# The k-slices of the split weights at 528 bytes instead of 512

## The chip, the cores and the metric

The kernel runs on one core of one Trainium2 chip. What counts is the device time of one execution in microseconds, as the median of several runs. A profile is one further execution, recorded instruction by instruction.

## The reference, cut to what matters

The program computes two residual layers on 512 positions of 1,024 channels in float32: an even layer (a chunked state-space scan beside differential attention), an odd layer (a diagonal state-space model beside latent attention), and a gated feed-forward after each. Nearly all of the work is projections `h @ w` with large weight matrices:

```python
def swiglu(x, wg, wu, wd):
    return (jax.nn.silu(x @ wg) * (x @ wu)) @ wd

for i in range(DEPTH):
    hn = rms_norm(h, norm_mix[i])
    h = h + (even_mixer(hn, ...) if i % 2 == 0 else odd_mixer(hn, ...))
    h = h + swiglu(rms_norm(h, norm_ffn[i]), ffn_gate[i], ffn_up[i], ffn_down[i])
return rms_norm(h, norm_final)
```

## The kernel before

Activations lie transposed: a tile of 128 channels by 512 positions, 2,048 bytes in each partition. The eight tiles of a layer's input are each held as a high part and a low part (`x0h`, `x0l` to `x7h`, `x7l`) whose sum is the float32 value, and the weights are split in the same way, so that three matmuls in the faster float32r format (high by high, high by low, low by high) stand for one float32 product.

The work comes in units. A unit is one block of 128 output channels (a few have 32 or 16): its weights are `nk` k-slices of `cw` columns, mostly 8 slices of 128. `wload` (line 154) brings the weights of one or more units into a tile `raw` with one DMA on SyncE's queue. `wsplit` (line 161) makes two tiles: `whi`, a cast on ScalarE (line 169), and `wlo`, raw minus high on VectorE (line 170). Both are allocated as 1,024 floats (4,096 bytes) from a pool `whl` with two buffers for each name, and slice k of 128 columns starts at 512 k bytes. In the last stage some weights are used twice and are kept in tiles of their own (`kh`, `kl`, 896 floats). `mm3` (line 173) issues three matmuls for each slice, lines 178, 179 and 180, with the slice as the stationary operand and 512 (at the end 256) positions as the moving one. In `v_part` (line 738) and `values` (line 1355) the slices are the moving operand.

`drive` (line 244) sets the order: before a unit's matmuls are issued, `prep` (line 192) issues the split of the next unit, so that ScalarE and VectorE work on it beside TensorE. `compute` (line 205) issues the matmuls and the unit's evacuation from PSUM, and then what is due from a queue of steps that are put off by a number of units. `even`, `ffn` and `odd` (lines 479, 936, 1217) give the units of the layers and the steps between them.

Memory is given out pool by pool in the order in which `setup` (line 370) and the layers open them. A pool `pad` of 320 floats, of which one is set by a memset on GpSimd (line 380), stands ahead of the residual tiles, the activation tiles, `raw` and `whl`; the layers' own pools come behind `whl`.

Of the kernel before, what the change touches and what calls it, by code (L numbers as in the profile page):

```python
# [9 lines left out]
F32 = mybir.dt.float32  # L10
F32R = mybir.dt.float32r
# [3 lines left out]
ALU = mybir.AluOpType  # L15
# [3 lines left out]
P = 128  # L19
# [2 lines left out]
KD = D // P  # L22
EPS = 1e-6
PAD, PAD5 = 320, 112
FFN = 2816
NH = FFN // P
MAGIC = 12582912.0
# [94 lines left out]
class Trunk:  # L122
# [38 lines left out]
    def wsplit(self, raw, o, nk, cw, keep=None):  # L161

        nc = self.nc
        n = nk * cw
        if keep is None:
            hi, lo = (self.t(self.whl, [P, 1024], x, F32R) for x in ("whi", "wlo"))
        else:
            hi, lo = (self.t(self.finp, [P, n], f"{x}{keep}", F32R) for x in ("kh", "kl"))
        nc.scalar.copy(out=hi[:, :n], in_=raw[:, o:o + n])  # L169
        nc.vector.tensor_tensor(out=lo[:, :n], in0=raw[:, o:o + n], in1=hi[:, :n].bitcast(F32), op=ALU.subtract)  # L170
        return [x[:, :n].rearrange("p (k c) -> p k c", k=nk) for x in (hi, lo)]

    def mm3(self, ps, hi, lo, k0, xs, m, start=True, stop=True):
        nc = self.nc
# [195 lines left out]
    def setup(self):  # L370
        nc, ctx = self.nc, self.ctx
        cp = self.cp = self.pool(ctx, "const")
        self.stp = self.pool(ctx, "stp")
        pad = self.pool(ctx, "pad")
        self.hp = self.pool(ctx, "hp")
        self.xnp = self.pool(ctx, "xnp")
        self.tmp = self.pool(ctx, "tmp")
        self.wraw = self.pool(ctx, "wraw", 2)
        self.whl = self.pool(ctx, "whl", 2)
        nc.gpsimd.memset(self.t(pad, [P, PAD], "pad")[:, 0:1], 0.0)  # L380
        self.pp = {n: self.pool(ctx, "ps_" + n, b, PSUM) for n, b in (("mm", 2), ("sc", 2), ("tp", 2), ("po", 2))}
        self.n_unit = 0
        self.raws, self.kept = {}, {}
        self.queue, self.held = [], None
        self.cst_sb = self.t(cp, [P, NCST], "cst")
        self.par_sb = self.t(cp, [P, NPAR], "par")
        nc.scalar.dma_start(out=self.par_sb, in_=self.a["par"])
        nc.scalar.dma_start(out=self.cst_sb, in_=self.a["cst"])
        self.ident = self.cst("ident")
        self.ones = self.t(cp, [P, P], "ones")  # L390
        nc.gpsimd.memset(self.ones, 1.0)
        self.mrow = self.t(cp, [1, P], "mrow", BF16)
        nc.gpsimd.memset(self.mrow[:, 0:64], 1.0)
        nc.gpsimd.memset(self.mrow[:, 64:128], 0.0)
        self.nrow = self.t(cp, [1, 64], "nrow", BF16)
        nc.gpsimd.memset(self.nrow, NEG)
        self.rowb = self.t(cp, [P, 32], "rowb")
        nc.scalar.dma_start(out=self.rowb, in_=self.a["rowp"].broadcast_to([P, 32]))
        self.sel = self.t(cp, [64, 16], "sel", F32R)
        nc.scalar.copy(out=self.sel, in_=self.cst("sel")[0:64, :])  # L400
        self.halfpi = self.t(cp, [P, 1], "hpi")
        nc.gpsimd.memset(self.halfpi, math.pi / 2)
        self.h = [self.t(self.hp, [P, T], f"h{i}") for i in range(KD)]
        self.xn = [None] * KD
# [1216 lines left out]
```

## Time and profile before

| | |
|---|---|
| median of 3 runs | 1480.8 us (1479.17 to 1481.18) |
| profiled execution | 1481.41 us |
| its span, from the first to the last instruction | 1479.6 us |
| mean granted TensorE clock | 0.986 |
| busy: TensorE, VectorE, ScalarE, GpSimd | 96%, 64%, 45%, 17% |
| chain that ended last: TensorE, VectorE, ScalarE, GpSimd | 74%, 18%, 3%, 2% |

Busy time is the union of an engine's instructions. TensorE's matmuls are pipelined: one is recorded as 0.39 us long while the next one starts 0.23 us after it, so the distance of the starts says more than the length. Weight loads are recorded apart, as PEld. The chain is followed back from the last instruction: at each step to what released it, or to the instruction before it on its engine.

### The profile page before, as it was taken

The page shows a single profiled execution, that of the slowest core. Times are in us where ns is not written, and L with a number is a line of the kernel's source. Part 1 is how long each engine was busy: PE and PEld are TensorE (multiplying, and loading weights), DVE is VectorE, ACT ScalarE, POOL GpSimd, SP SyncE. Part 2 cuts the span into 40 slices and gives each one's busy share as a digit, 9 for nine tenths or more (in the row PEclk, how much of TensorE's full clock was granted, in tenths as well). Part 3 has the DMA queues.
Part 4 walks back from the last instruction along what each step waited for, and adds up shares of the span by engine and source line. Part 5 has one row for each costly group of instructions (what it writes and reads, how often), then busy time and mean ns, then how long its engine had stood idle before and what let it go on. Part 6 is the DMA issues. An engine that isn't in the chain of part 4 may idle for free.

```text
span 1479.6 us, 18488 instructions
## 1 busy us (share of the span) xinstructions
PE 1426.2 (96%) x7043; PEld 1155.1 (78%) x7043; DVE 954.1 (64%) x1992; ACT 661.5 (45%) x1198; POOL 256.9 (17%) x206
## 2 busy tenths in 40 slices
PE   7999999999999999999999997789999999999997
PEld 5877877788878877888888886666688888888887
DVE  6987788777664999774634469886664433443453
ACT  5658766767544334334223453256453322222342
POOL 0234511000002210011011213523221100100111
PEclk9999999999999999999999998889999999999999
DMA  5221121112212222223222221020122232323221
GB/s 179 78 73 58 61 82 44 59 57 72 86 58 85 102 86 86 86 86 107 96 103 87 98 86 38 24 75 2 62 109 85 89 112 86 108 77 114 86 100 57
DMA packets 20248, 119.80 MB, mean 81 GB/s; under 512 B 2368, under 2 KB 3008, under 8 KB 9024
## 3 DMA queue, kind: packets, MB, share of 16 engines
q1 hardware_dynamic: 18864, 116.86, 22.9%
q10 hardware_dynamic: 1296, 1.76, 0.4%
q8 instruction: 55, 0.90, 0.3%
q14 instruction: 33, 0.27, 0.1%
HBM read 116.52 MB, written 2.10 MB: 80 GB/s over the span
## 4 chain that ended last, share of the span: by engine, by line
PE 74%; DVE 18%; ACT 3%; POOL 2%; issue 2%; DMA 1%; SPq 0%; ACTq 0%; DVEq 0%; POOLq 0%
PE mm L178 14%; PE mm L180 14%; PE mm L179 13%; PE sc L180 7%; PE sc L179 7%; PE sc L178 7%; DVE wlo L170 3%; PE sc L1397 1%; PE sc L813 1%; POOL xs L281 1%; PE po L842 1%; DVE qsw L608 1%; PE mm L750 1%; PE po L1425 1%; PE sc L812 1%
## 5 line engine op out<-in xcount | busy, mean ns | idle before, releaser
L169 ACT CAST whi<-raw 128x1024 fp32r<-128x1024 f32 (+5 forms) x231 | 223.9, 970 | 568.6 <-PE mm L179 331.3
L170 DVE TENSOR_TENSOR wlo<-raw,whi 128x1024 fp32r<-128x1024 f32 (+5 forms) x231 | 266.8, 1155 | 44.2 <-ACT whi L169 31.6
L281 POOL TENSOR_TENSOR gt<-gt,rbc 128x512 f32<-128x512 f32 x44 | 76.3, 1734 | 572.6 <-ACT gt L952 572.6
L957 DVE TENSOR_TENSOR gt<-mm,gt 128x512 f32<-128x512 f32 x44 | 30.3, 690 | 111.3 <-PE mm L180 107.9
L281 POOL TENSOR_TENSOR sacc<-sacc,sq 128x512 f32<-128x512 f32 x29 | 45.4, 1566 | 300.5 <-issue 232.7
L951 DVE TENSOR_TENSOR gt<-sc,rbc 128x512 f32<-128x512 f32 x44 | 30.3, 689 | 88.9 <-PE sc L180 88.9
L180 PE MATMUL mm<-x0h,wlo 128*128 128x512 f32 (+2 forms) x91 | 37.2, 409 | 12.4 <-DVE wlo L170 12.4
L178 PE MATMUL mm<-x0h,whi 128*128 128x512 f32 (+2 forms) x91 | 39.9, 438 | 6.1 <-ACT x0h L343 5.4
L972 DVE TENSOR_TENSOR h<-h,mm 128x512 f32<-128x512 f32 x20 | 13.7, 687 | 44.0 <-PE mm L180 44.0
L768 ACT ACTIVATE qsw<-mm 32x512 f32<-32x512 f32 x64 | 37.7, 589 | 3.1 <-DVE qraw L764 2.3
L972 DVE TENSOR_TENSOR h<-h,sc 128x512 f32<-128x512 f32 x20 | 13.7, 686 | 38.9 <-PE sc L180 38.8
L178 PE MATMUL mm<-x1h,whi 128*128 128x512 f32 (+2 forms) x91 | 36.7, 403 | 1.8 <-ACT x1h L343 1.8
L952 ACT ACTIVATE gt<-gt 128x512 f32<-128x512 f32 x44 | 27.6, 628 | 22.9 <-DVE gt L951 22.9
L180 PE MATMUL mm<-x1h,wlo 128*128 128x512 f32 (+2 forms) x91 | 37.3, 410 | 0.0
L180 PE MATMUL mm<-x2h,wlo 128*128 128x512 f32 (+2 forms) x91 | 37.2, 408 | 0.0
L178 PE MATMUL mm<-x7h,whi 128*128 128x512 f32 (+2 forms) x95 | 37.1, 391 | 0.0
L180 PE MATMUL mm<-x7h,wlo 128*128 128x512 f32 (+2 forms) x95 | 37.1, 391 | 0.0
L179 PE MATMUL mm<-x7l,whi 128*128 128x512 f32 (+2 forms) x95 | 37.0, 390 | 0.0
L179 PE MATMUL mm<-x0l,whi 128*128 128x512 f32 (+2 forms) x91 | 36.8, 405 | 0.2 <-DVE x0l L344 0.2
L179 PE MATMUL mm<-x2l,whi 128*128 128x512 f32 (+2 forms) x91 | 37.0, 407 | 0.0
L179 PE MATMUL mm<-x1l,whi 128*128 128x512 f32 (+2 forms) x91 | 36.8, 404 | 0.2 <-DVE x1l L344 0.2
L178 PE MATMUL mm<-x3h,whi 128*128 128x512 f32 (+2 forms) x91 | 36.8, 405 | 0.0
(938 smaller groups left out, 4385.5 us busy)
## 6 DMA issues: line engine op xcount, KB each, us to landing
raw<-in_f_dram SPq DMA_DIRECT2D x52, 1024.0 KB, 4.8
raw<-in_w_dram SPq DMA_DIRECT2D x35, 1024.0 KB, 4.8
raw<-in_f_dram SPq DMA_DIRECT2D x16, 896.0 KB, 4.5
raw<-in_w_dram SPq DMA_DIRECT2D x8, 512.0 KB, 3.6
h<-in_xt_dram SPq DMA_DIRECT2D x8, 256.0 KB, 6.8
raw<-in_w_dram SPq DMA_DIRECT2D x2, 640.0 KB, 3.9
out_dram<-otm SPq DMA_DIRECT2D x4, 256.0 KB, 2.5
out_dram<-otm ACTq DMA_DIRECT2D x4, 256.0 KB, 2.9
```

What stands on the lines that cost most here:

```text
L169: nc.scalar.copy(out=hi[:, :n], in_=raw[:, o:o + n])
L170: nc.vector.tensor_tensor(out=lo[:, :n], in0=raw[:, o:o + n], in1=hi[:, :n].bitcast(F32), op=ALU.subtract)
L178: nc.tensor.matmul(ps, lhsT=hi[:, k, :m], rhs=xh, start=start and j == 0, stop=False)
L179: nc.tensor.matmul(ps, lhsT=hi[:, k, :m], rhs=xl, start=False, stop=False)
L180: nc.tensor.matmul(ps, lhsT=lo[:, k, :m], rhs=xh, start=False, stop=stop and j == n - 1)
L281: self.nc.gpsimd.tensor_tensor(out=out, in0=x, in1=y, op=op)
L608: V.scalar_tensor_tensor(out=acc, in0=xr[:, 1 + k:1 + k + T], scalar=self.par("cw", 12 * k + j), in1=acc, op0=ALU.mult, op1=ALU.add)
L768: A.activation(out=sw[c * 32:(c + 1) * 32, :], in_=ps[d * 32:(d + 1) * 32, :], func=AF.Identity, scale=scale)
L951: V.tensor_tensor(out=gt, in0=ps, in1=E["rbc"], op=ALU.mult)
L952: A.activation(out=gt, in_=gt, func=AF.Silu)
L957: V.tensor_tensor(out=gt, in0=ps, in1=gt, op=ALU.mult)
L972: V.tensor_tensor(out=self.h[i], in0=self.h[i], in1=ps, op=ALU.add)
```

## The change

A constant `WGAP` of 4 floats, 16 bytes, is added behind each k-slice in `whi` and `wlo`: slices of 128 columns lie 528 bytes apart, those of 256 columns 1,040. The low parts start 32 floats, 128 bytes, into their tile. The tiles grow to 1,056 and 1,088 floats. ScalarE and VectorE write through a view in three dimensions that leaves the gaps out. The kept tiles stay as they were, written through a view of the same contiguous memory. A new pool `padw` of 320 floats behind `whl`, with a memset of one value on GpSimd, makes the two pools together 2,048 bytes longer than `whl` was.

```diff
+WGAP = 4
@@ wsplit
         if keep is None:
-            hi, lo = (self.t(self.whl, [P, 1024], x, F32R) for x in ("whi", "wlo"))
+            w = nk * (cw + WGAP)
+            hi, lo = (self.t(self.whl, [P, 1024 + 8 * WGAP + s], x, F32R)[:, s:s + w].rearrange(
+                "p (k c) -> p k c", k=nk)[:, :, :cw] for x, s in (("whi", 0), ("wlo", 8 * WGAP)))
         else:
-            hi, lo = (self.t(self.finp, [P, n], f"{x}{keep}", F32R) for x in ("kh", "kl"))
-        nc.scalar.copy(out=hi[:, :n], in_=raw[:, o:o + n])
-        nc.vector.tensor_tensor(out=lo[:, :n], in0=raw[:, o:o + n], in1=hi[:, :n].bitcast(F32), op=ALU.subtract)
-        return [x[:, :n].rearrange("p (k c) -> p k c", k=nk) for x in (hi, lo)]
+            hi, lo = (self.t(self.finp, [P, n], f"{x}{keep}", F32R).rearrange("p (k c) -> p k c", k=nk)
+                      for x in ("kh", "kl"))
+        src = raw[:, o:o + n].rearrange("p (k c) -> p k c", k=nk)
+        nc.scalar.copy(out=hi, in_=src)
+        nc.vector.tensor_tensor(out=lo, in0=src, in1=hi.bitcast(F32), op=ALU.subtract)
+        return hi, lo
@@ setup
         nc.gpsimd.memset(self.t(pad, [P, PAD], "pad")[:, 0:1], 0.0)
+        nc.gpsimd.memset(self.t(self.pool(ctx, "padw"), [P, 320], "padw")[:, 0:1], 0.0)
```

## Rows read from the trace of the kernel before

**Rows 1.** The page: busy time by engine; the chain that ended last, by engine and line.

```profile
PE 1426.2 (96%) x7043; PEld 1155.1 (78%) x7043; DVE 954.1 (64%) x1992; ACT 661.5 (45%) x1198; POOL 256.9 (17%) x206
...
PE 74%; DVE 18%; ACT 3%; POOL 2%; issue 2%; DMA 1%; SPq 0%; ACTq 0%; DVEq 0%; POOLq 0%
PE mm L178 14%; PE mm L180 14%; PE mm L179 13%; PE sc L180 7%; PE sc L179 7%; PE sc L178 7%; DVE wlo L170 3%; PE sc L1397 1%; PE sc L813 1%; POOL xs L281 1%; PE po L842 1%; DVE qsw L608 1%; PE mm L750 1%; PE po L1425 1%; PE sc L812 1%
```

**Rows 2.** Busy time by stretch: length, then busy and instructions by engine, TensorE clock, DMA.

```profile
core 0: us, PE busy (x) PEld busy (x) DVE busy (x) ACT busy (x) POOL busy (x), PEclk, DMA share, GB/s
100.00:300.00 200.00, 194.72 (x1080) 155.44 (x1078) 157.45 (x320) 147.92 (x271) 51.69 (x36) 0.97 0.17 59
1200.00:1300.00 100.00, 100.00 (x443) 82.87 (x442) 37.62 (x42) 25.18 (x30) 10.82 (x6) 1.00 0.27 94
```

**Rows 3.** Matmuls in order of time, second feed-forward: start and length in us.

```profile
1305.04 0.39 PE L178 MATMUL mm<-x0h,whi 128*128 128x512 f32 x1
...
1310.25 0.39 PE L180 MATMUL mm<-x7h,wlo 128*128 128x512 f32 x1
1310.48 0.39 PE L178 MATMUL sc<-hid0h,whi 128*128 128x512 f32 x1
```

**Rows 4.** Weight loads in order of time: 128 columns, then 32 columns.

```profile
1305.04 0.19 PEld L179 LDWEIGHTS mm<-x0l,whi 128*128 128x128 f32 x1
...
948.56 0.11 PEld L178 LDWEIGHTS mm<-x3h,whi 128*32 128x32 f32 x1
```

**Rows 5.** Matmuls of 256 columns in the last stage, in order of time.

```profile
1440.06 0.28 PE L180 MATMUL mm<-hid3h,kl 128*128 128x256 f32 x1
...
1441.14 0.29 PE L180 MATMUL mm<-hid6h,kl 128*128 128x256 f32 x1
```

**Rows 6.** Matmuls in order of time after a break of TensorE, first layer.

```profile
102.11 0.39 PE L179 MATMUL mm<-x0l,whi 128*128 128x512 f32 x1
...
104.41 0.39 PE L180 MATMUL mm<-x3h,wlo 128*128 128x512 f32 x1
...
107.13 0.39 PE L180 MATMUL mm<-x7h,wlo 128*128 128x512 f32 x1
```

**Rows 7.** Matmuls with 32 weight columns, in order of time.

```profile
947.63 0.40 PE L179 MATMUL mm<-x1l,whi 128*32 128x512 f32 x1
...
952.01 0.39 PE L180 MATMUL mm<-x7h,wlo 128*32 128x512 f32 x1
```

**Rows 8.** Groups by shape, the split: busy us, mean ns of one, idle before.

```profile
L169 ACT CAST whi<-raw 128x1024 fp32r<-128x1024 f32 x174 | 182.5, 1049 | 456.1 <-PE mm L179 264.0 <-PE sc L179 159.9 <-PE mm L751 14.3
L169 ACT CAST whi<-raw 128x512 fp32r<-128x512 f32 x20 | 12.4, 620 | 23.0 <-PE mm L179 20.6 <-DVE b L1382 1.3 <-ACT sq L276 0.6
L170 DVE TENSOR_TENSOR wlo<-raw,whi 128x1024 fp32r<-128x1024 f32 x174 | 218.1, 1253 | 39.3 <-ACT whi L169 28.6 <-PE tp L326 9.8
```

**Rows 9.** Groups by shape, other operations for comparison.

```profile
L1026 DVE COPY otm<-tp 128x256 f32<-128x256 f32 x16 | 6.7, 419 | 1.2 <-PE tp L1025 1.1
L1002 DVE TENSOR_TENSOR h<-h,mm 128x256 f32<-128x256 f32 x14 | 5.9, 420 | 21.6 <-PE mm L180 21.6
L603 DVE TENSOR_TENSOR qraw<-mm,rbc 128x512 f32<-128x512 f32 x10 | 6.8, 682 | 0.0
L951 DVE TENSOR_TENSOR gt<-sc,rbc 128x512 f32<-128x512 f32 x44 | 30.3, 689 | 88.9 <-PE sc L180 88.9
L1447 ACT CAST t<-us 128x512 fp32r<-128x512 f32 x4 | 4.3, 1102 | 1.3 <-DVE us L1443 1.3
```

**Rows 10.** Waits of TensorE for the split: us in total, times, longest.

```profile
PE mm L180 <- DVE wlo L170: 15.7, 7, 6.1
```

**Rows 11.** GpSimd's memset at the start, and TensorE's first matmul, in order of time.

```profile
0.71 0.10 POOL L380 MEMSET pad<- 128x1 f32 x1 [0.29 <-POOLq L1611]
...
5.41 0.61 PE L178 MATMUL mm<-x0h,whi 128*16 128x512 f32 x1 [5.41 <-ACT x0h L343]
```

**Rows 12.** Line 178 over the whole span; columns as in rows 2, TensorE alone.

```profile
0.00:1480.00 1480.00, 673.27 (x1715) 324.51 (x1715) 0.99 0.24 81
```

## The prediction, made before the change was run

> **What bounds the kernel now.** I read the page first. TensorE is busy for 96% of the span and makes 74% of the chain that ended last, and six of the seven costliest lines of that chain are the matmuls of lines 178 to 180; VectorE has 18%, of which the low parts of the split (line 170) are 3% [rows 1]. The stretches say where the two matter: in the second feed-forward TensorE is busy all the time and VectorE for 38 of 100 us; in the first layer VectorE works 157 of 200 us and TensorE has short breaks [rows 2]. The change moves the places in memory from which lines 178 to 180 read their weights, so the question is what sets the distance from one matmul to the next.
>
> From the order of time: 24 matmuls of one unit, with eight k-slices of high parts and eight of low parts, take from 1305.04 to 1310.48, so 5.44 / 24 = 0.2267 us each [rows 3]. Matmuls of 256 columns stand (1441.14 - 1440.06) / 9 = 0.1200 us apart [rows 5]. The two give 106.7 ns for 256 columns, 0.417 ns a column, which is the 2.4 GHz level (the granted clock is 1.00 there), and a fixed part of 120.0 - 106.7 = 13.3 ns in each matmul whatever its width. The weight load takes 0.19 us, beside the matmul before [rows 4]. After a break the distance is larger for a while: (104.41 - 102.11) / 10 = 230 ns for the first ten, then (107.13 - 104.41) / 12 = 226.7 [rows 6].
>
> **The change part by part.** The span is 1479.6 us in a profiled execution of 1481.4, so 1.8 us lie around it; that execution is 0.6 above the median of the runs, 1480.8. A difference under 0.2%, about 3 us, can't be told from no change here.
>
> *Matmuls.* Lines 178 to 180 issue 3 x 1715 = 5,145 of them [rows 12]. Their number, shapes, order and waits stay. Only the addresses of the weights change: slice k starts 16 k bytes further than before, the low parts 128 more, against data tiles of 2,048 bytes that keep their places relative to each other. No row of before has 128-column weights at such places. The nearest rows are those where the places differ already. Within a unit the slice goes through eight steps of 512 bytes and two tiles, and the distances are equal [rows 3]. The kept tiles of the last stage are other tiles again, of 3,584 bytes, and give the same 13.3 ns [rows 5]. The nearest to the change is the unit with 32 weight columns, whose slices lie 128 bytes apart, off the grid of 512: (952.01 - 947.63) / 19 = 230.5 ns [rows 7]. That is 3.8 ns more than 226.7, but its load is short too (0.11 us against 0.19 [rows 4]), and it begins after a break, where 230 is usual [rows 6]. So per matmul the cost lies between +3.8 ns (rows 7 taken whole) and -13.3 ns (the whole fixed part gone): between +19.6 and -68 us. I take 0, by rows 3 and 5, because many different places there give one distance.
>
> *High parts, line 169, ScalarE.* 231 casts write rows of 128 with a hole of 16 bytes behind each, where they wrote one run; 1,049 ns for 1,024 values [rows 8]. No row shows ScalarE writing so. Upper end: line 1447 reads with a jump at every value and takes 1,102 ns against 620 for a contiguous cast of the same size [rows 8, 9], 482 / 512 = 0.94 ns a jump; seven jumps are 6.6 ns. Paying that price at every value is excluded, since only seven of the 1,023 steps jump and the others go to the neighbour. Lower end: 0, since no value is saved. I take 0 to 7 ns. ScalarE is 45% busy and 3% of the chain [rows 1]: 44 us x 7 / 1,049 = 0.3 us at the most.
>
> *Low parts, line 170, VectorE.* Same number of values, 1,253 ns [rows 8]. Line 1026 writes 256 values in two runs in 419 ns, line 1002 writes 256 in one run in 420 [rows 9]. Line 603 writes at 16 bytes into its tile in 682 ns, line 951 at a tile's start in 689 [rows 9]. So neither runs nor a shift of 16 bytes cost VectorE anything: between 0 and -7 ns. At -7 ns on the 3% of the chain, 44 us x 7 / 1,253 = -0.25 us; I take 0. If the cover were gone, TensorE's waits for line 170 would show it: 15.7 us in seven waits now [rows 10]; no queue has an instruction more in front of them.
>
> *GpSimd and memory.* One memset of one value, as that of line 380: 0.10 us at 0.71, before TensorE's first matmul at 5.41, which waits for ScalarE [rows 11]. It is hidden by the loading of the input; without that cover it would cost 0.1 us. The weights' pool grows by 768 bytes and the new pad has 1,280, together 2,048: every later tile moves by that, and to each other and to the data tiles in front they lie as before modulo 2,048. No DMA is added, and SyncE's queue keeps its order.
>
> Sum: 1481.4 + 0.3 - 0.25 + 0 = 1481.4 for an execution like the profiled one, 1481 against the median.
>
> **A rule of the Trainium skill against the row.** By "TensorE: Matmul & The Clock Gate", section "Back-to-back issue gap", an isolated matmul of N columns at the full clock is followed after N / 2.4 + 2.5 ns, 216 ns for 512. The trace has 226.7 [rows 3]; were the difference of 10.8 ns all a matter of addresses, and were it to go, an estimate from that page would be 5,145 x 10.8 = 56 us less, 1425. By "SBUF — State Buffer", section "Who interferes with whom", TensorE reads weights and data through two independent ports and waits for nobody, so moving the weights would do nothing; that speaks against the change, and rows 4 and 7, where a shorter load brings no shorter distance, agree with it as far as they go.
>
> **The rivals.** *Faster, by the fixed part.* The loads of the next weights run beside the matmul [rows 3, 4], and the 13.3 ns do not grow with the columns, as a meeting of the load with the data would not. All 128-column slices of before lie a multiple of 512 bytes from one another, so rows 3 and 5 can't exclude that the grid itself costs it. Against it: the load of 32 columns reads a quarter as much, and the distance is no shorter [rows 4, 7]. At 5.1 us for each ns it decides from 0.6 ns; half of the fixed part gone gives 34 us, 1447.
>
> *Faster, a little: the state after a break.* If the 230 ns after a break come from such meetings and the new places end them, 10 x 3.3 ns = 33 ns are saved a break. With at most one break to a unit of 24, 5,145 / 24 = 214, that is 7 us at the most: 1474. Against: most units of the feed-forwards follow without a break [rows 2, 3].
>
> *Slower: the state after a break stays.* The places of before may be the ones at which load and data fall into step, which they do after ten matmuls [rows 6]; off the grid they didn't within 20 [rows 7]. If the new places keep all of the 5,145 at 230.5 ns, that is 3.8 ns each, 19.6 us, 1501; at half of it 1491. It decides from 0.6 ns per matmul. For it: rows 7 is the one stretch with slices off the grid. Against: its loads are short and the stretch is brief.
>
> *The change doesn't do what it says.* Slices of 256 columns come to 1,040 bytes apart, and the kept tiles stay at 512; but these are few beside the 128-column ones [rows 12], so this can't take the effect away. The order of the program could come out otherwise with the added memset; nothing in the rows gives that a sign, and it belongs to the forecast's width.
>
> **How the numbers follow.** Forecast, no address matters: 0.50, 1481 (1478 to 1484). The state after breaks goes: 0.14, 1474. Part of the fixed 13.3 ns goes: 0.13, 1447. The state after a break stays: 0.18, 1491 to 1501. A longer split on ScalarE and VectorE that eats into rows 10: 0.05, 1485. So faster 0.27, within 0.2% 0.50, slower 0.23. The range goes from 1468 to 1498: it takes in the smaller gain and most of the loss, and leaves out the large gain (0.13) and the top of the loss (0.05).
>
> **What the changed profile would show.** If I am right: 24 matmuls of a unit in the second feed-forward in 5.44 us, 0.120 us at 256 columns, 230 after a break falling to 226.7, line 169 at 1,049 to 1,056 ns and line 170 at 1,253, and the waits of rows 10 near 15.7 us. A first rival shows as a distance under 226 in the feed-forward; the second as 226.7 from the first matmul after a break; the third as 228 to 231 in the feed-forward, with TensorE's busy time there still 100 of 100 us. I am wrong if the distance in the feed-forward moves by more than 0.6 ns.

## The result, and the profile after

The changed kernel takes 1498.5 us (median of 4 runs, 1497.9 to 1501.1), the kernel before, on the same chip, 1480.0 (4 runs): a ratio of 1.0128, 95% interval [1.011, 1.0145], so 18.5 us slower. The forecast was 1481, the range ended at 1498. What came true is the third rival, nearly at its full size (1501). The profiled execution took 1498.7 us, with a span of 1496.9 and a granted clock of 0.988, against 0.986 in the profiled execution of before, so the loss doesn't come from the clock.

The page of the changed kernel, busy time by engine and the chain that ended last (answers [rows 1]):

```profile
PE 1445.7 (97%) x7043; PEld 1153.2 (77%) x7043; DVE 955.9 (64%) x1992; ACT 662.2 (44%) x1198; POOL 256.6 (17%) x207
...
PE 76%; DVE 17%; ACT 3%; POOL 2%; issue 2%; DMA 0%; SPq 0%; DVEq 0%; ACTq 0%; POOLq 0%
PE mm L183 14%; PE mm L185 14%; PE mm L184 14%; PE sc L185 7%; PE sc L184 7%; PE sc L183 7%; DVE wlo L175 2%; PE sc L1403 1%; PE sc L819 1%; POOL xs L286 1%; PE po L848 1%; DVE qsw L614 1%; PE mm L756 1%; PE po L1431 1%; PE sc L818 1%
```

Only TensorE has grown: 1445.7 us busy instead of 1426.2, with the same 7,043 matmuls. The weight loads (1153.2, before 1155.1), VectorE and ScalarE are within 2 us of before. `mm3` has lines 183 to 185 here, the split lines 174 and 175.

Busy time by stretch, columns as in [rows 2]:

```profile
1200.00:1300.00 100.00, 100.00 (x432) 80.83 (x431) 37.51 (x41) 24.29 (x28) 8.50 (x6) 1.00 0.27 95
```

TensorE is busy for all of the 100 us, as before, and starts 432 matmuls instead of 443: it doesn't wait for anybody, each matmul takes longer. Matmuls in order of time say how much (start and length in us):

```profile
1303.03 0.39 PE L183 MATMUL sc<-x0h,whi 128*128 128x512 f32 x1
...
1308.61 0.40 PE L183 MATMUL mm<-x0h,whi 128*128 128x512 f32 x1
...
1314.20 0.39 PE L183 MATMUL sc<-x0h,whi 128*128 128x512 f32 x1
...
1321.64 0.19 PEld L183 LDWEIGHTS mm<-x3h,whi 128*128 128x128 f32 x1
```

24 matmuls of a unit take 5.58 and 5.59 us, 232.7 ns each, where [rows 3] have 5.44 us and 226.7 ns. The recorded weight load is as long as in [rows 4], 0.19 us; the loss stands between the starts of the matmuls, and the load's own row doesn't show it.

After a break in the first layer (answers [rows 6]), and the kept tiles of the last stage, whose places the change left alone (answers [rows 5]):

```profile
102.14 0.40 PE L183 MATMUL mm<-x2h,whi 128*128 128x512 f32 x1
...
104.45 0.40 PE L184 MATMUL mm<-x5l,whi 128*128 128x512 f32 x1
...
106.09 0.40 PE L185 MATMUL mm<-x7h,wlo 128*128 128x512 f32 x1
...
1451.83 0.28 PE L185 MATMUL mm<-hid3h,kl 128*128 128x256 f32 x1
...
1452.91 0.29 PE L185 MATMUL mm<-hid6h,kl 128*128 128x256 f32 x1
```

Ten matmuls soon after the break stand 2.31 / 10 = 231 ns apart, as in [rows 6], but the next seven 1.64 / 7 = 234 ns: the fall to 226.7 doesn't come. The kept tiles have 1.08 / 9 = 120.0 ns as before.

The split by shape (answers [rows 8]):

```profile
L174 ACT CAST whi<-raw 128x1024 fp32r<-128x1024 f32 x174 | 182.0, 1047 | 472.1 <-PE mm L184 279.1 <-PE sc L184 165.5 <-PE mm L757 14.0
L175 DVE TENSOR_TENSOR wlo<-raw,whi 128x1024 fp32r<-128x1024 f32 x174 | 217.9, 1253 | 37.1 <-ACT whi L174 22.4 <-PE tp L331 10.1
```

TensorE's waits for it (answers [rows 10]):

```profile
PE mm L185 <- DVE wlo L175: 14.5, 7, 6.0
```

1,047 and 1,253 ns against 1,049 and 1,253, waits of 14.5 us against 15.7: writing rows with holes costs the two engines nothing that these rows show.

Where the 17.3 us between the two spans lie can be added up, since both programs issue the same 7,043 matmuls in the same order. Taking the distance from each matmul's start to the next in both traces: 4,565 distances between matmuls of lines 183 to 185 with 512 positions that follow each other without a break have grown by 23.2 us in all (5.1 ns each); 189 distances with a break have shrunk by 7.3 us; all others have grown by 0.6 us; the first matmul starts 0.7 us later. The 7.3 us are not all the work of the change. Twenty of these distances stood at about 427 ns before, which is the lower level of the clock (512 columns at 1.2 GHz), and at 226 to 252 ns after; that alone is 3.9 us. In both traces TensorE had stood still for over 6 us at 891 and for about 3 at 908 us. From 912 to 916 us, before and after (length, busy time and matmuls of TensorE, granted clock, DMA):

```profile
912.00:916.00 4.00, 4.00 (x12) 0.57 0.11 18
912.00:916.00 4.00, 4.00 (x28) 1.00 0.00 0
```

Another 2.0 us are one wait at 6.6 us, while the input is loaded. About 2 us are left for what a TensorE that is late waits less for the others. Two kernels below with the distances of before have breaks that are 3.4 and 5.1 us shorter than those of before, and 1.9 and 3.2 us of that are again distances at the lower clock level: the trace of before has 61 of them, the most of all 15 traces here (the others have 39 to 58).

### The profile page after: what moved, and what is told of

It reads as the page before. It is cut to its first block, busy times and chain, and to the rows that moved or that the text cites. A ratio compares the mean times of both kernels' runs of the same rounds, so it can differ in the third digit from the quotient of the medians.

```text
span 1496.9 us, 18489 instructions
## 1 busy us (share of the span) xinstructions
PE 1445.7 (97%) x7043; PEld 1153.2 (77%) x7043; DVE 955.9 (64%) x1992; ACT 662.2 (44%) x1198; POOL 256.6 (17%) x207
## 4 chain that ended last, share of the span: by engine, by line
PE 76%; DVE 17%; ACT 3%; POOL 2%; issue 2%; DMA 0%; SPq 0%; DVEq 0%; ACTq 0%; POOLq 0%
PE mm L183 14%; PE mm L185 14%; PE mm L184 14%; PE sc L185 7%; PE sc L184 7%; PE sc L183 7%; DVE wlo L175 2%; PE sc L1403 1%; PE sc L819 1%; POOL xs L286 1%; PE po L848 1%; DVE qsw L614 1%; PE mm L756 1%; PE po L1431 1%; PE sc L818 1%
## 5 line engine op out<-in xcount | busy, mean ns | idle before, releaser
L183 PE MATMUL mm<-x2h,whi 128*128 128x512 f32 (+2 forms) x91 | 37.2, 409 | 0.0
```

Of the source, the lines that this page charges most:

```text
L183: nc.tensor.matmul(ps, lhsT=hi[:, k, :m], rhs=xh, start=start and j == 0, stop=False)
```

## The experiments

All are compared with the kernel before, run on the same chip. Below, the *place* of a weight slice is its address modulo 256 bytes, where the data tiles are on multiples of 256, as they are before and after (all data tiles that `mm3` streams lie on such multiples, and before so do all slices of 128 columns). After the change the slices' places run over all sixteenths: 16 k or 16 k + 128 for the high parts, since the second buffer lies 128 bytes off as well, and 16 k + 128 for the low ones. A distance is from a matmul's start to the next one's, for 512 positions, the first twelve after a break (a distance over 250 ns) left out. Before, it is 226.6, 226.8 and 226.6 ns on lines 178, 179 and 180.

The first four kernels set three theories against each other. *Places*: what counts is where the weights lie. *Writes*: ScalarE's and VectorE's rows with holes disturb TensorE's reads. *Moved pools*: the later tiles, 2,048 bytes further, cost it.

**The low parts 128 bytes off, no gap.** Edit to the changed kernel:

```
-WGAP = 4
+WGAP, LOFF = 0, 32
-... for x, s in (("whi", 0), ("wlo", 8 * WGAP)))
+... for x, s in (("whi", 0), ("wlo", LOFF)))
-... self.pool(ctx, "padw"), [P, 320], "padw") ...
+... self.pool(ctx, "padw"), [P, 448], "padw") ...
```

> One part alone: the slices lie 512 bytes apart as before, only the low parts start 128 bytes into their tile (the pad behind is 448 floats, so that the two pools are again 2,048 bytes longer). Places theory (the distance of two matmuls depends on where the weights being loaded lie, modulo 512, against the data): two matmuls of three load from a place that is off the grid or change the place, so the distance in the second feed-forward is 228 to 233 ns and the time 1485 to 1500. Writes theory (the writes in runs with holes disturb TensorE): nothing is written with holes here, 226.7 ns and 1480. Moved-pools theory (what counts is that the later tiles lie 2,048 bytes further): 232 ns and 1498, as the whole change.

Measured: 1488.0 us, ratio 1.0059 [1.0044, 1.0074]. The two buffers of `wlo` are 4,224 bytes apart here, so that the low parts have place 128 in one and 0 in the other. Two units in a row, in order of time:

```profile
1298.61 0.39 PE L183 MATMUL mm<-x0h,whi 128*128 128x512 f32 x1
...
1304.05 0.39 PE L183 MATMUL sc<-x0h,whi 128*128 128x512 f32 x1
...
1309.60 0.39 PE L183 MATMUL mm<-x0h,whi 128*128 128x512 f32 x1
```

The unit with its low parts at place 0 takes 5.44 us, the one at place 128 5.55. In the latter the three distances are 226.7, 232.5 (the low slice is loaded) and 234.2 ns (the one after it), in the former 226.7 each. That is one kernel with the same writes and the same moved pools in both units, so both other theories fall as causes of the loss. 604 distances at 234.2 and 629 at 232.5 ns, 7.5 and 5.8 ns too long, are 8.2 us, most of the 9.

**The gap of 16 bytes alone**, low parts at the start of their tiles (`WGAP, LOFF = 4, 0` in the same edit, `padw` 384):

> The other part alone: gaps of 16 bytes behind the slices, the low parts at the start of their tile (the pad behind is 384 floats). Places theory: the place moves by 16 bytes a slice, high and low alike, 228 to 233 ns and 1485 to 1500. Writes theory: all of the loss, 232 ns and 1498. Moved-pools theory: 232 ns and 1498.

Measured: 1498.5 us, 1.0135 [1.0118, 1.0151], and 432 matmuls in the stretch from 1200 to 1300, as in the changed kernel. The gap brings the whole loss without the 128 bytes, though these alone bring 9 us: the two don't add up.

**Slices of high and low parts by turns, on multiples of 512.** Edit to the kernel before: one tile for both, written in runs of 128 values with holes of 512 bytes.

```
-hi, lo = (self.t(self.whl, [P, 1024], x, F32R) for x in ("whi", "wlo"))
+hl = self.t(self.whl, [P, 2048], "whl", F32R)[:, :2 * n].rearrange("p (k s c) -> p k s c", k=nk, s=2)
+hi, lo = hl[:, :, 0, :], hl[:, :, 1, :]
```

> Writes in runs without leaving the grid: high and low slices of a unit lie by turns in one tile of 2,048 floats, so that every slice of 128 columns starts at a multiple of 512 bytes, and ScalarE and VectorE write runs of 128 with holes of 512 bytes. No pool moves. Places theory: 226.7 ns and 1480, as before. Writes theory: 232 ns and 1498 or more. Moved-pools theory: 226.7 ns and 1480.

Measured: 1482.3 us, 1.003 [1.0019, 1.0041]; distances 226.7, 226.7 and 226.6 ns. Writes with holes do nothing to TensorE. The small loss isn't in the matmuls' distances. In the profile the granted clock is 0.93 from 1000 to 1100 us, where before has 1.00. But the profiled execution, 1487.1 us, was the slowest of seven, 4.9 above the median, so this stretch tells of that excess and not of the 3 us at the median. TensorE's matmuls also come in another order at 198 of 7,043 places. What makes the 3 us was not tried and stays open.

**A scan of places.** Edit to the kernel before: both parts of split u (u = 0 to 230) start 16 x (u mod 32) bytes into their tiles, slices 512 bytes apart.

```
+s = 4 * (self.n_split % 32)
+self.n_split += 1
-hi, lo = (self.t(self.whl, [P, 1024], x, F32R) for x in ("whi", "wlo"))
+hi, lo = (self.t(self.whl, [P, 1024 + 128], x, F32R)[:, s:s + n] for x in ("whi", "wlo"))
```

> A map of the places: slices 512 bytes apart, high and low parts of unit number u both 16 x (u mod 32) bytes into their tile, written in one run; later tiles move by 2,048 bytes. Within a unit all loads come from one place modulo 512. Places theory, if the place itself counts: the distance within a unit is a function of the offset, 226.7 ns at 0 and up to 236 elsewhere, perhaps under 226 at some. Places theory, if only the change from one place to the next counts: 226.7 ns in every unit after its first few matmuls, and the time near 1482. Writes theory: 226.7 everywhere. Moved-pools theory: 232 ns in all units.

Measured: 1496.0 us in its one execution. The mean distance by place, some 200 to 270 distances each (places 256 bytes apart gave the same within 0.7 ns and are put together):

```
place   0     16    32    48    64    80    96    112
ns      226.9 228.3 233.2 233.2 233.1 231.8 233.9 233.3
place   128   144   160   176   192   208   224   240
ns      233.3 233.3 233.4 230.0 229.0 233.1 233.2 227.8
```

The period is 256 bytes, place 0 is the best of the 16, and most others cost 6 to 7 ns.

The next three ask whether the weights' own address counts or its relation to the data's, and whether 256 is all that is needed.

**Data and weights 128 bytes further.** Edit to the kernel before: `PAD` 352 instead of 320.

> From the kernel before; a pad in front of the data tiles is 128 bytes longer, so that the data tiles and the weight tiles alike lie 128 bytes past a multiple of 256 and their relation is that of before. The scan of places gave 226.8 ns a matmul for weights on a multiple of 256 with the data on one, and 233.2 for weights 128 bytes off it. Relation theory (what counts is where the weights lie against the data that stream beside their load, modulo 256 bytes): 226.7 ns, the time of before, 1479 us within 2. Own-place theory (what counts is where the weights alone lie): 233 ns, some 20 us more, 1497 to 1500 us.

Measured: 1479.3 us, 1.0001 [0.9991, 1.0011], distances 226.7, 226.6, 226.7 ns. Own-place theory falls: the scan has 233.3 ns for weights at that address with the data left where they were.

**The data x0h to x7l 64 bytes further, weights on multiples of 256.** Edit to the kernel before: `PAD` 336, and a pool of 496 floats ahead of `wraw`.

> From the kernel before; the weights stay on multiples of 256 bytes, the data tiles x0h to x7l (3,282 of the 5,145 matmuls stream from them) move 64 bytes on, the other data tiles (hid and the rest, 1,833 matmuls) stay on multiples of 256. Relation theory: the weights now lie 64 bytes short of the data, which is place 192 of the scan, 229.0 ns beside 226.8: the x matmuls go to about 229 ns, the rest keeps 226.7, the time rises by 3,282 x 2.2 ns = 7 us to some 1486 us. If the relation counted the other way round (place 64 of the scan, 233.1 ns): x matmuls 233 ns, 1499 us. Own-place theory: 226.7 ns everywhere and 1479 us.

Measured: 1483.2 us, 1.0026 [1.0013, 1.0038]. Two units, one streaming from the moved tiles (24 matmuls) and one from `hid`, which was not moved (21):

```profile
1307.61 0.39 PE L178 MATMUL mm<-x0h,whi 128*128 128x512 f32 x1
...
1313.10 0.40 PE L178 MATMUL sc<-hid0h,whi 128*128 128x512 f32 x1
...
1317.91 0.39 PE L178 MATMUL mm<-hid0h,whi 128*128 128x512 f32 x1
...
1322.67 0.39 PE L178 MATMUL sc<-hid0h,whi 128*128 128x512 f32 x1
```

5.49 / 24 = 228.8 ns against 4.76 / 21 = 226.7. Weights 64 bytes short of the data are place 192 of the scan, 229.0 ns; so the relation counts, and with this sign. The distances add 6.4 us by the trace, near the expected 7; the time rose by less, 2.9 us between the medians and 3.9 by the ratio. In its trace 4.2 us come back in distances that stood at the lower clock level in one of the two, as above.

**Slices 768 bytes apart, low parts 256 bytes into their tiles.** The changed kernel with `WGAP, LOFF = 64, 64`:

> The changed kernel with a gap of 256 bytes in place of 16 between the slices (they lie 768 bytes apart) and the low parts 256 bytes into their tiles: the same form of code, all weights on multiples of 256 bytes and half of them off multiples of 512. Period-256 theory: 226.7 ns and the time of before, 1479 to 1482 us; the whole loss is gone although gap and shift are larger. If it were the gaps as such, or if multiples of 512 were wanted: at least half of the loss stays, 1488 to 1498 us.

Measured: 1479.3 us, 0.9998 [0.9989, 1.0008]; matmuls in order of time:

```profile
1296.74 0.39 PE L183 MATMUL sc<-x0h,whi 128*128 128x512 f32 x1
...
1302.18 0.39 PE L183 MATMUL mm<-x0h,whi 128*128 128x512 f32 x1
```

5.44 us a unit. The same code with gaps and shift sixteen times and twice as large is as fast as before: only what is left modulo 256 costs.

The next three move one operand at a time by 128 bytes, to see which meeting costs: *pairing* says that a distance grows when the load beside a stream lies off that stream.

**Only the low data tiles**, **only the high data tiles** (tiles of `T + 64` floats, of which `[:, 32:32 + T]` is used, for `x0l` to `x7l` or `x0h` to `x7h`), **only the high weights** (tiles of 1,088 floats, `whi` from the 32nd on); edits to the kernel before.

> From the kernel before; only the low data tiles x0l to x7l move 128 bytes off the multiple of 256 (1,094 of the matmuls stream from one); weights and high data stay on it. Pairing theory (a distance grows when the weights loaded beside a stream lie off that stream): only the distance from the matmul hi*xl to lo*xh grows, to 232 to 233 ns; 1,094 x 6 ns = 6.6 us, 1485. Carry-over theory (as with the low parts 128 bytes off, where the distance after the odd load grew as well): hi*xl to lo*xh and the one after it both grow, 1,094 x 13 ns = 14 us, 1492. Own-place theory of the weights: no distance grows.

> From the kernel before; only the high data tiles x0h to x7h move 128 bytes off (2,188 matmuls stream from one). Pairing theory: the distances from hi*xh to hi*xl and from lo*xh to the next hi*xh grow to 232 to 233 ns, the one from hi*xl to lo*xh stays at 226.7; 2,188 x 6 ns = 13 us, 1492. Carry-over theory: all three grow or two of them by more, 15 to 20 us, 1494 to 1499.

> From the kernel before; only the high weights move 128 bytes off, low weights and all data stay on multiples of 256. Pairing theory: the distances during which high weights are loaded grow, lo*xh to hi*xh and hi*xh to hi*xl, to 232 to 233 ns, and hi*xl to lo*xh stays at 226.7; 3,050 x 6 ns = 18 us, 1497. Carry-over theory: all three grow, 20 us or more, 1499 and above.

Measured: 1488.5 us, 1.0063 [1.004, 1.0086]; 1485.5, 1.0051 [1.0031, 1.0071]; 1502.2, 1.0158 [1.0129, 1.0188]. The distances of the matmuls that stream from the x tiles, in ns, with the two kernels above beside them:

```
128 bytes off            hi*xh  hi*xl  lo*xh  sum of three
nothing (before)         226.6  226.8  226.6  680.0
high data                232.4  226.0  228.4  686.8
low data                 229.9  233.0  228.6  691.5
  of it, 502 of 778      227.1  233.0  226.8  687.0
  of it, 276 of 778      234.8  233.3  231.4  699.4
low weights (place 128)  226.7  232.5  234.2  693.4
high weights             232.3  232.7  235.0  700.0
both weights (scan)                           699.9
```

The row of the low data is a mean of two kinds of stretches: of 778 threes of distances, 500 add up to 686 to 689 ns and 274 to 698 to 700, and only four lie elsewhere. Two units of this kernel, one of each kind:

```profile
655.34 0.40 PE L178 MATMUL mm<-x0h,whi 128*128 128x512 f32 x1
660.94 0.40 PE L178 MATMUL sc<-x0h,whi 128*128 128x512 f32 x1
...
1304.35 0.39 PE L178 MATMUL sc<-x0h,whi 128*128 128x512 f32 x1
1309.84 0.39 PE L178 MATMUL mm<-x0h,whi 128*128 128x512 f32 x1
```

5.60 / 24 = 233.3 and 5.49 / 24 = 228.8 ns. In the larger part pairing holds to the letter: only the distance from `hi*xl` grew, by 6.2 ns. It falls by the other kernels: with the high data moved, one of the two distances that should have grown by 6 ns grew by 1.8; with the high weights moved, the one that should have stayed grew by 6; with the low weights moved, the one behind the odd load grew by 7.6. The carry-over theory, which has the distance after an odd load grow as well, fits the low and the high weights. It doesn't fit the data: with the low data one or all three distances grew where it had two, and for the high data it expected 1494 to 1499 us. So neither theory covers the four. In the two kernels with moved data the matmuls that stream from `hid`, which stayed, kept 226.7 to 227.0 ns.

**A finer scan**, the code of the first with steps of 4 bytes: `s += 56 if s < 16 else 88`, in floats.

> From the kernel before; as in the scan of places both parts of a unit's weights start off the grid, here in steps of 4 bytes: 16 places from 224 to 284 (32 short of a multiple of 256 to 28 past it) and 16 from 416 to 476 (160 to 220 past one), from split to split. Grid theory: 226.7 ns is the least that a place can give, every place from 240 to 272 gives 226.7 to 228, the others 228 to 233.5; some 12 us above before, 1491. Rival, that part of the 13.3 ns at each matmul is a meeting of load and data as well: some place gives less than 226 ns, and a kernel with all its weights there would be faster than before, 5 us for each ns.

Measured: 1503.7 us in its one execution, 12 above the expectation. Place 0 has 227.5 ns and no place is below 226.7; but places 4 to 28 lie at 230.6 to 234.5, and 212 at 236.0: there is no smooth dip around 0. Place 204 has 226.7 only if distances over 250 ns are counted as breaks. Two of its six units, at 214 and 842 us, don't hold 226.7: in them every seventh distance is 254 or 255 ns, and the mean is 234 to 235. The second, 21 distances in order of time:

```profile
841.59 0.42 PE L181 MATMUL sc<-hid0h,whi 128*128 128x512 f32 x1
...
846.53 0.40 PE L181 MATMUL mm<-hid0h,whi 128*128 128x512 f32 x1
```

4.94 / 21 = 235 ns; with these two place 204 has 228.6. The expectation for this place below rests on the reading without them. And place 16 has 233.3 ns, where the first scan had 228.3. By units the two agree: at place 16 every unit stands either at 226.7 or at 233.3 ns, from its seventh matmul on without exception. In the first scan eight units of fourteen had 226.7, in the finer one none of five. So the place isn't all: it seems to allow certain steady distances, and something else, perhaps what went before, decides which is taken. Two more kernels put this to the test.

**All weights at place 16**, and **all weights at place 204**:

```
-hi, lo = (self.t(self.whl, [P, 1024], x, F32R) for x in ("whi", "wlo"))
+hi, lo = (self.t(self.whl, [P, 1024 + 64], x, F32R)[:, 4:4 + 1024] for x in ("whi", "wlo"))
```

(51 in place of 4 for place 204.)

> From the kernel before; all parts of the split start 16 bytes past a multiple of 256, the slices 512 bytes apart, the data on multiples of 256. In the first scan eight of eleven units at this place stood at 226.7 ns, all of them behind units at place 0; three that began otherwise, and five of five in the finer scan, stood at 233.3. Settled-state theory: at this place no break ends in 226.7, so 233.3 ns stays, some 4,250 x 6 ns less what the waits give back, 1497 to 1501 us; a few stretches at 226.7 may occur. Place theory (the place alone decides; the first scan's mean of 228.0 ns holds): 228 ns and 1483 to 1486 us.

> From the kernel before; all parts of the split start 204 bytes past a multiple of 256, the slices 512 bytes apart, the data on multiples of 256. In the finer scan every unit at this place stood at 226.7 ns from its first six matmuls on, where units at place 0 began at 227 to 232 ns after a break. Settled-state theory (load and data fall into one of a few steps, and a place decides how soon and into which): 226.7 ns throughout, the slower start of the units goes, up to 4,565 x 0.6 ns = 2.7 us less than before, 1476 to 1479. Grid theory (only multiples of 256 give 226.7): 229 to 233 ns and 1490 to 1500 us.

Measured at place 16: 1490.2 us, 1.0068 [1.0049, 1.0088], in executions from 1483.3 to 1492.7, where before spreads from 1477.6 to 1480.7. Two stretches of one execution, in order of time, each 44 matmuls from its first line to its second:

```profile
346.60 0.40 PE L178 MATMUL mm<-bc,whi 128*128 128x512 f32 x1
...
356.87 0.39 PE L180 MATMUL mm<-x7h,wlo 128*128 128x512 f32 x1
...
389.39 0.39 PE L178 MATMUL mm<-bc,whi 128*128 128x512 f32 x1
...
399.37 0.39 PE L180 MATMUL mm<-x7h,wlo 128*128 128x512 f32 x1
```

10.27 / 44 = 233.4 ns and 9.98 / 44 = 226.8 ns, with the same shapes, the same data tiles, the same places and a granted clock of 1.00 in both; both go through the pool's two buffers, 4,352 bytes (17 x 256) apart, and differ only in which comes first. Of the 51 unbroken stretches of 20 or more distances in this trace, 33 stand at 233.3 and 18 at 226.7, each for its whole length after the first twelve; the longest, of 1,387 distances, at 226.7. Before has 52 such stretches, and all 52 end at 226.7. So the settled-state theory holds in its core, and the place alone doesn't decide. My number for it was wrong: I had all breaks end in 233.3. The traced execution, 1485.3 us with 228.0 ns on the mean, meets the number of the place theory, but as a mix of 226.7 and 233.3, which that theory doesn't have.

Measured at place 204: 1510.7 us, 1.0209 [1.0194, 1.0224], the slowest of all. Matmuls in order of time:

```profile
1300.06 0.42 PE L178 MATMUL sc<-x1h,whi 128*128 128x512 f32 x1
...
1305.01 0.42 PE L178 MATMUL mm<-x0h,whi 128*128 128x512 f32 x1
```

21 distances take 4.95 us, 236 ns each; single ones take 255 ns. One unit of the whole trace, that at 84 us, holds 226.7 ns. Of the finer scan's six units at this place four had 226.7 ns, and I had taken them for all. Both theories missed the time, the settled-state one by 32 us.

No place of the weights gave a mean distance under 226.6 ns, and no kernel here beats the one before.

## Why the prediction was wrong

*What bounds the kernel* was right: the distance of lines 178 to 180 is what the time hangs on, and the time rose with it at 100 of 100 us busy.

*The matmul term* is the step that failed: "I take 0, by rows 3 and 5, because many different places there give one distance". The many places of [rows 3, 5] were one place: multiples of 512 bytes for the weights and for the data, place 0 every time. They could tell nothing about the change, which leaves these multiples. The one row off them, [rows 7] with 230.5 ns, was named as the nearest and then set aside for its short load and its break. The measured growth, 5.1 ns, lies above the bound of 3.8 ns taken from it; 4,565 distances times 5.1 ns less what the breaks gave back makes the 17.3 us between the two spans, where 5,145 x 3.8 ns made 19.6. That the third rival's 1501 lies so near is partly luck: the growth was larger than its 3.8 ns, the matmuls with it fewer. That [rows 7] showed the same thing isn't shown: its 12 matmuls at place 128 are too few, and those at place 0 between them have 224 to 235 ns too.

*The third rival* ("the places of before may be the ones at which load and data fall into step, which they do after ten matmuls; off the grid they didn't") had the mechanism in the main. It lacked that other places settle as well, mostly at 233.3 ns. Place 0 is special in that every stretch ends in step there: 52 of 52 before, and 53 of 53 both with everything moved by 128 bytes and with slices 768 bytes apart. I gave it 0.18 because I counted its evidence as brief; the stretch was brief, but it was the only one.

*The two faster rivals*: the fixed 13.3 ns stayed at every place, so it isn't a meeting that any place tried here removes. The state after a break isn't ended by the change; the distances stay as long as there, or longer.

*High and low parts* were right in that nothing was lost: -2 and 0 ns, against 0 to 7 and 0 to -7. The *memset* and the *moved pools* were right: the kernel with 768 bytes has both, and equals before.

*The rule of the Trainium skill*, "SBUF — State Buffer", section "Who interferes with whom", has TensorE read weights and data through independent ports without waiting, from which I had that moving weights does nothing. The runs differ: 226.7 ns at place 0, about 233 at most others, and moving both operands by the same 128 bytes gives 226.7 again.

*The range* ended at 1498 and left out "the top of the loss". The bound of the unknown cost, 3.8 ns times all matmuls, reached to 1501, and the range should have taken it in.

What stays open is which accesses meet. That the distance depends on the weights' place against the data's, modulo 256 bytes, is shown, and that it isn't the place alone. That it is the load of the next weights beside the stream is only argued, and the pairing tried for it fell; what picks the steady distance after a break wasn't tried.

## What to carry to other kernels

In matmuls of the shape used here, keep the slices that TensorE loads and the tiles that it streams beside them on the same address modulo 256 bytes; a pad or a gap that isn't a multiple of 256 cost up to 3% of each matmul (at place 204, 4%), and only the starts of the matmuls show it, not the load's row. When rows "with different addresses" are to show that addresses don't matter, work out first in which respect they differ. Where one row stands off the pattern, it bounds the unknown better than many rows on it. And look at how distances are spread before taking their mean: three means here were mixes of two levels, and a limit that sorts out breaks can sort out the effect.

## What was not expected of the hardware

- Steady distances come in steps of about 6.7 ns: 226.7 and 233.3 for one matmul, and for three 680.0, 686.8, 693.4 and 700.0. At place 204 they aren't steady: the units above have seven distances that recur, 235 ns on the mean. At 0.417 ns a column [rows 3, 5], 6.7 ns are 16 columns; the 13.3 ns of place 0 are 32.
- A distance has a memory: at place 16 a stretch holds 226.7 or 233.3 ns from its start to its end, over up to 1,387 distances. The executions spread over 9 us, where those of before spread over 3; that this comes from which stretches hold which distance is likely, but only one was traced.
- After a break the first six distances are 231 ns on the mean before, and fall to 226.7; at place 16 a stretch that holds 226.7 has 227.1 in its first six.
